# Storing two of three row tiles of an encoder step through 32x32 squares turned on VectorE, in 128-byte runs, instead of through TensorE transposes

## The chip, the core and the metric

The kernel runs on one core of one Trainium2 chip. A core has five engines with queues of their own: TensorE (PE, matrix products, with weight loads listed as PEld), VectorE (DVE), ScalarE (ACT), GpSimd (POOL) and SyncE (SP, which here only issues DMAs). Each engine works its queue in order; semaphores order the engines among each other. DMAs are issued from SP's, ACT's or POOL's queue and run on 16 DMA engines that all queues share. The metric is the device time of one execution, in microseconds (us); lower is better.

## The reference

Two groups of rows go through the same two layers with the same weights: a prompt of 1024 rows and a sample of 32 rows, each row 1024 wide, all in float32.

```python
def trunk(x, c, pool_cache, ...):
    for i in range(DEPTH):                         # DEPTH = 2
        mod = jax.nn.silu(c) @ w_ada[i] + b_ada[i]
        sh1, sc1, gt1, sh2, sc2, gt2 = jnp.split(mod[:, None, :], N_MOD, axis=-1)
        h = rmsnorm(x, g_norm[i, 0]) * (1 + sc1) + sh1
        ...                                        # layer 0: gated MLP over chunks, layer 1: pooling
        x = x + gt1 * rmsnorm(mix, g_norm[i, 1])
        h = rmsnorm(x, g_norm[i, 2]) * (1 + sc2) + sh2
        f = jnp.square(jax.nn.relu(h @ ffn_w_up[i])) @ ffn_w_down[i]
        x = x + gt2 * rmsnorm(f, g_norm[i, 3])
    return x, sgu_states, pool_states
```

What matters here is the very end: the last line of layer 1 for the prompt's first 768 rows, and how these rows get from the core's memory to `y_prompt` (1, 1024, 1024).

## The kernel before, in words

**Layout.** The 1056 rows are cut into three tiles (`TILES`): tile 0 and tile 1 with 384 prompt rows each, tile 2 with 256 prompt rows and the 32 sample rows (288 columns). On the core everything is held transposed: `acc[t]` is 128 partitions x 8 blocks x rows, so that column `r` of block `k` holds channels `128k` to `128k + 127` of row `r`. `A(t, k)` is block `k` of it.

**The FFN.** The hidden width 4096 is cut into eight chunks of 512 (`c` from 0 to 7). `ffn_item` does one chunk for one tile: four up blocks (`pf`, 24 matmuls each) whose results go through ACT (relu L1368, square L1370, a rounded copy `fh` L1192) and DVE (the rest `fl`), and then eight down blocks (`pg`, 12 matmuls each, three for each of four hidden blocks), each of which DVE adds to `acc`. Every product takes three matmuls (L932 to L934): high part by high part, by low part, and low by high. The down half of an item is held back and put behind the first up block of the next item (`pending`, `flush`), so that ACT and DVE have time for `fh` and `fl`. A weight comes in by an SP DMA into one of three `raw` buffers, ACT makes the high part `wh`, DVE the low part `wl`.

**The last passes.** In layer 1 chunks 6 and 7 are done for tiles 0 and 1 first and for tile 2 alone afterwards. So the results of tiles 0 and 1 can be stored while tile 2's last two chunks run, and only tile 2's own end stands at the end of the kernel.

**Fillers.** Work that is not on the main path is written as generators. `to_out` adds one per tile (`out_0`, `out_1`, `out_2`) as soon as that tile's last chunk is done. `weave` takes steps from the fillers whenever a running estimate of DVE's time is behind one of PE's (`time`, `tick`, `on_dve`); `yield 0.5` closes a filler for that long by the same estimate, `yield True` asks for the next step at once. The order within each engine's queue is then set by the framework from this program order and its own estimates.

**The end of tiles 0 and 1.** `residual` (L821) scales and adds: it reads the old `x` back from memory (`xd`, L828) and leaves the final result in `acc[t]`, still transposed. Then, for each of three blocks of 128 rows, eight 128x128 matmuls against the identity turn it on PE (L1700, into PSUM tiles `yT`), ACT copies the halves into a `raw` buffer `yo` (L1701), and SP stores 128 rows of 4 KB (L1702).

**The end of tile 2** has a path of its own (`last`). Its `acc` is turned on PE as it becomes ready (`turn_last`, L1449). The old `x` comes back in row order: `mix_to_ffn` had written it to `xtd`, `load_last` (L1423) reads it in runs of 128 bytes, and `turn_x` turns it in 32x32 squares on DVE. Four additions on DVE and four stores on SP finish the prompt rows (L1677, L1678). For the 32 sample rows ACT scales (L1682, `zlast`), POOL adds (L1683, `xlast`) and ACT's queue stores (L1684).

**Rooms.** `room("h", t)` and `room("l", t)` are the two large buffers of a tile; each new tile of that name waits until the one before it is no longer used. `hh` and `hl`, the FFN's inputs, live there.

**Other users of the queues touched.** Before this point POOL has done little: four DMAs at the start (`load_vectors`, L192) and eight memsets in layer 0. SP carries the weight loads (L436), the residual's reads (L828) and `load_last`.

Of the kernel before, what the change touches and what calls it, by code (L numbers as in the profile page):

```python
# [11 lines left out]
AF = mybir.ActivationFunctionType  # L12
# [3 lines left out]
P = 128  # L16
D = 1024
KB = D // P
# [5 lines left out]
HALO = 16  # L24
NV = 2

TILES = [(0, 384, 0), (384, 384, 0), (768, 256, DEC)]
# [7 lines left out]
def tile_stream_encoder_step(  # L35
# [25 lines left out]
    nc = tc.nc  # L61
    act = nc.scalar.activation
# [6 lines left out]
    def tick(us):  # L69
        time["pe"] += us  # L70
        time["dve"] = max(time["dve"], time["pe"] - 4.0)

    def on_dve(op, fixed, rate):
        def run(out, *args, **kw):
            n = 1
            for k in out.shape[1:]:
                n *= k
            time["dve"] += fixed + n / rate
            return op(out, *args, **kw)  # L79

        return run
# [4 lines left out]
    turn32 = on_dve(nc.vector.transpose, 0.1, 930.0)  # L86

    def pool(name, **kw):
# [14 lines left out]
    acc = [const.tile([P, KB, HALO + n], F32, name=f"acc{t}") for t, n in enumerate(ncol)]  # L103
# [7 lines left out]
    ident = const.tile([P, P], F32, name="ident")  # L111
# [6 lines left out]
        out=quad, in_=ident.rearrange("p (c m) -> p m c", m=32), op=ALU.add, axis=AX.X  # L118
# [9 lines left out]
    def A(t, kb, c0=0, w=None):  # L128
        w = ncol[t] - c0 if w is None else w
        return acc[t][:, kb, HALO + c0 : HALO + c0 + w]  # L130


    def room(part, t, name, dtype=F32):
        return work.tile([P, KB, ncol[t]], dtype, tag=f"h{part}{t}", bufs=1, name=name)
# [4 lines left out]
    def ps_dn(name):  # L139
        return psum.tile([P, 512], F32, tag="pd", bufs=3, name=name)  # L140

    def ps_ms(name):
        return psum.tile([P, 512], F32, tag="pm", bufs=3, name=name)
# [10 lines left out]
    def t_st(name):  # L154
        return work.tile([P, 4], F32, tag="st", bufs=6, name=name)
# [6 lines left out]
    def t_x(name, shape):  # L162
        return work.tile(shape, F32, tag="x3", bufs=3, name=name)

    def t_raw(name):
        return work.tile([P, 1024], F32, tag="raw", bufs=RAW_SLOTS, name=name)
# [501 lines left out]
    def need_ada(l, which):  # L668
        k = max(ada_last[(l, which * 4 + i)] for i in range(4))
        while state["next"] <= k:  # L670
            assert stream_ready()
            stream_step()
        run_deferred(True)
# [147 lines left out]
    def residual(st, l, cf, tag, out, store=True, stat=True):  # L821
        t = st.t
        n = ncol[t]
        xos = {}

        def load(k2):
            xos[k2] = t_x(f"xo_{tag}_{k2}", [P, 2, n])
            nc.sync.dma_start(xos[k2], xd[t][:, 2 * k2 : 2 * k2 + 2, :])  # L828

        got = []  # L830
        yield from st.finish(got)
        r = got[0]
        st2 = Stat(t, tag + "x")
        for half in range(2):
            for k2 in (2 * half, 2 * half + 1):
                load(k2)
            for k2 in (2 * half, 2 * half + 1):
                for k in (2 * k2, 2 * k2 + 1):
                    for c0, w, v in segs[t]:
                        a = A(t, k, c0, w)  # L840
                        stt(
                            out=a,
                            in0=a,
                            scalar=coef[:, l, cf, v, k : k + 1],
                            in1=r[:, c0 : c0 + w],
                            op0=ALU.mult,
                            op1=ALU.mult,
                        )
                    yield True
                a = acc[t][:, 2 * k2 : 2 * k2 + 2, HALO:]  # L850
                tt(out=a, in0=a, in1=xos[k2], op=ALU.add)
                if stat:
                    st2.square(2 * k2, a)
                yield k2 % 2 == 0
        if store:
            nc.sync.dma_start(xd[t], acc[t][:, :, HALO:])
        out.append(st2)
# [585 lines left out]
    def turn_last(d):  # L1443
        half = d // 4
        for i, (c0, _, _) in enumerate(LAST):
            if d % 4 == 0:
                take = ps_up if half == 0 and i < 2 else (ps_ms if half == 0 or i < 2 else ps_dn)
                last_ps[(i, half)] = take(f"yT{i}_{half}")
            nc.tensor.transpose(  # L1449
                last_ps[(i, half)][:, (d % 4) * P : (d % 4 + 1) * P], A(NT - 1, d, c0, P), ident  # L1450
            )
# [182 lines left out]
    run_ffn(0, to_pool)  # L1634


    def to_out(st):
        t = st.t
        col0, npr, nsm = TILES[t]
        blocks = [  # L1640
            (c * P, P, y_prompt[0, col0 + c * P : col0 + (c + 1) * P, :]) for c in range(npr // P)
        ]
        if nsm:
            blocks.append((npr, nsm, y_sample[0]))

        def last():

            turn_last(KB - 2)
            pn = ps_dn("pn_last")
            nb = len(LAST)  # L1650
            for k in (0, KB - 1):
                if k > 0:
                    turn_last(KB - 1)
                for i, (c0, _, _) in enumerate(LAST):
                    mm(
                        pn[:, 2 * i : 2 * i + 2],
                        st.sq[:, k, c0 : c0 + P],
                        ones[:, 0:2],
                        start=k == 0 and i == 0,
                        stop=k > 0 and i == nb - 1,  # L1660
                        skip_group_check=True,
                    )
            sums = pn[:, : 2 * nb].rearrange("p (b c) -> p b c", c=2)[:, :, 0]
            r, q = (t_st(f"{x}_last")[:, :nb] for x in ("r", "q"))
            act(out=r, in_=sums, func=AF.Abs_reciprocal_sqrt, scale=1.0 / D)
            tt(out=q, in0=r, in1=r, op=ALU.mult)
            stt(out=q, in0=sums, scalar=-0.5 / D, in1=q, op0=ALU.mult, op1=ALU.mult)
            stt(out=r, in0=q, scalar=1.5, in1=r, op0=ALU.add, op1=ALU.mult)
            xt = last_ps["x"]
            dsts = [dst for _, _, dst in blocks]  # L1670
            for i, (_, r0, nr) in enumerate(LAST):
                rows = slice(r0, r0 + nr)
                for half in range(2):
                    d = slice(half * 512, half * 512 + 512)
                    y, x = last_ps[(i, half)][rows, :], xt[rows, i, d]
                    if nr == P:
                        stt(out=x, in0=y, scalar=r[rows, i : i + 1], in1=x, op0=ALU.mult, op1=ALU.add)  # L1677
                        nc.sync.dma_start(dsts[i][:, d], x)  # L1678
                        continue

                    z = t_x(f"zlast{half}", [P, 512])[rows, :]
                    act(out=z, in_=y, func=AF.Copy, scale=r[rows, i : i + 1])  # L1682
                    nc.gpsimd.tensor_tensor(out=x, in0=z, in1=x, op=ALU.add)  # L1683
                    nc.scalar.dma_start(dsts[i][:, d], x)  # L1684
            yield False

        def run():
            need_ada(1, 5)
            if t == NT - 1:
                yield from last()  # L1690
                return
            yield from residual(st, 1, 3, f"r2_1_{t}", [], store=False, stat=False)
            yield 0.5
            for c0, w, dst in blocks:
                tick(1.0)
                yo = t_raw(f"yo{t}_{c0}")
                for half in range(2):
                    pt = ps_ms(f"yT{t}_{c0}_{half}")
                    for i in range(4):
                        nc.tensor.transpose(pt[:w, i * P : (i + 1) * P], A(t, half * 4 + i, c0, w), ident)  # L1700
                    act(out=yo[:w, half * 512 : (half + 1) * 512], in_=pt[:w, :], func=AF.Copy)  # L1701
                nc.sync.dma_start(dst, yo[:w, :])  # L1702
                yield False

        fillers.append((f"out_{t}", run()))

    run_ffn(1, to_out)
    flush()
    for t in range(NT):
# [44 lines left out]
```

## Time and profile before

| | us |
|---|---|
| median of three runs | 2160.07 (2159.87 to 2161.8) |
| the profiled execution | 2160.34 |
| its span, first to last instruction | 2158.5 |
| ACT busy with L1701, tiles 0 and 1 | 6.35 |
| a PE transpose of L1700, mean length of the 48 | 0.276 |

The granted TensorE clock was 0.998 in this execution. A profile row gives an engine, a line, an operation and its operands as out<-in; times in a timeline are microseconds from the start of the span, first the start and then the length. On PE successive instructions overlap, so that the lengths add up to more than the time that passes; the distance between two starts is what an instruction takes from the queue. DVE's elementwise work goes through one helper and shows as L79.

### The profile page before, as it was taken

To read this page: it belongs to the slowest core of one execution; us is meant where nothing else is said; L and a number is where in the kernel's file an instruction comes from. 1 tells how busy PE (TensorE), PEld (TensorE's weight loads), DVE (VectorE), ACT (ScalarE), POOL (GpSimd) and SP (SyncE) were. 2 spreads that over 40 slices of the span, in tenths; PEclk is the share of its full clock that TensorE was granted. 3 is DMA by queue.
4 is the path that set the end of the run, shared out by engine and by line. 5 is a ranking of instruction groups with operands and counts; after the bars stand their busy time and mean duration, and the time that the engine had idled before them with its cause. 6 is when DMAs were issued, how large, how long until landed. Compare 5 with 4: busy or idle time off the path is not lost.

```text
span 2158.5 us, 33202 instructions
## 1 busy us (share of the span) xinstructions
PE 2140.5 (99%) x13186; PEld 2077.4 (96%) x13186; DVE 1428.4 (66%) x2531; ACT 982.7 (46%) x1667; POOL 7.9 (0%) x20
## 2 busy tenths in 40 slices
PE   8999999999999999999999999999999999999998
PEld 5878999999999999999999999999999999999998
DVE  6778838567778549576757779869684553523375
ACT  5634431233456652324345566656464542322454
POOL 0000000000000000000000000000000000000000
PEclk9999999999999999999999999999999999999999
DMA  8586524353446444334545466465454541302243
GB/s 289 163 259 208 181 82 136 97 163 109 121 134 213 128 146 147 101 114 141 178 125 162 147 194 198 145 193 164 141 164 131 165 149 57 108 20 69 79 137 120
DMA packets 372495, 311.78 MB, mean 144 GB/s; under 512 B 29842, under 2 KB 335290, under 8 KB 372340
## 3 DMA queue, kind: packets, MB, share of 16 engines
q1 hardware_dynamic: 372084, 309.43, 46.6%
q8 instruction: 103, 1.69, 0.3%
q14 instruction: 52, 0.43, 0.1%
q10 hardware_dynamic: 128, 0.14, 0.0%
q0 software_dynamic: 128, 0.09, 0.0%
HBM read 278.95 MB, written 30.66 MB: 143 GB/s over the span
## 4 chain that ended last, share of the span: by engine, by line
PE 97%; DVE 1%; DMA 1%; ACT 1%; issue 0%; POOL 0%; POOLq 0%; SPq 0%; ACTq 0%; DVEq 0%
PE pf L932 11%; PE pf L934 11%; PE pf L933 11%; PE pg L932 11%; PE pg L934 11%; PE pg L933 11%; PE pu L932 3%; PE pu L934 3%; PE pu L933 3%; PE po L932 3%; PE po L933 3%; PE po L934 3%; PE pv L958 2%; PE pv L960 2%; PE pv L959 2%; PE psp L1286 1%
## 5 line engine op out<-in xcount | busy, mean ns | idle before, releaser
L932 PE MATMUL pg<-fh,wh_dn 128*128 128x384 f32 (+1 forms) x1536 | 496.0, 323 | 0.0
L932 PE MATMUL pf<-hh,wh_up 128*128 128x384 f32 (+1 forms) x1536 | 494.4, 322 | 0.0
L934 PE MATMUL pf<-hh,wl_up 128*128 128x384 f32 (+1 forms) x1536 | 493.0, 321 | 1.2 <-DVE wl_up L79 1.2
L933 PE MATMUL pf<-hl,wh_up 128*128 128x384 f32 (+1 forms) x1536 | 493.1, 321 | 0.0
L933 PE MATMUL pg<-fl,wh_dn 128*128 128x384 f32 (+1 forms) x1536 | 492.5, 321 | 0.0
L934 PE MATMUL pg<-fh,wl_dn 128*128 128x384 f32 (+1 forms) x1536 | 492.5, 321 | 0.0
L79 DVE TENSOR_TENSOR wl_up<-raw,wh_up 128x1024 fp32r<-128x1024 f32 x152 | 186.0, 1224 | 169.9 <-ACT wh_up L449 167.5
L449 ACT ACTIVATE wh_up<-raw 128x1024 fp32r<-128x1024 f32 x152 | 161.1, 1060 | 283.9 <-PE pf L933 218.1
L934 PEld LDWEIGHTS pf<-hh,wl_up 128*128 128x128 f32 x1536 | 288.6, 188 | 1.9 <-DVE wl_up L79 1.9
L932 PEld LDWEIGHTS pg<-fh,wh_dn 128*128 128x128 f32 x1536 | 288.3, 188 | 1.3 <-ACT fh L1192 0.4
L933 PEld LDWEIGHTS pg<-fl,wh_dn 128*128 128x128 f32 x1536 | 288.3, 188 | 0.9 <-DVE fl L79 0.2
L933 PEld LDWEIGHTS pf<-hl,wh_up 128*128 128x128 f32 x1536 | 288.3, 188 | 0.4
L932 PEld LDWEIGHTS pf<-hh,wh_up 128*128 128x128 f32 x1536 | 288.2, 188 | 0.4
L934 PEld LDWEIGHTS pg<-fh,wl_dn 128*128 128x128 f32 x1536 | 288.3, 188 | 0.0
L79 DVE TENSOR_TENSOR acc<-acc,pg 128x384 f32<-128x384 f32 (+1 forms) x336 | 174.2, 519 | 150.5 <-PE pg L934 149.8
L449 ACT ACTIVATE wh_dn<-raw 128x1024 fp32r<-128x1024 f32 x152 | 160.9, 1060 | 207.9 <-PE pg L933 170.6
L79 DVE TENSOR_TENSOR wl_dn<-raw,wh_dn 128x1024 fp32r<-128x1024 f32 x152 | 186.0, 1224 | 82.0 <-ACT wh_dn L449 81.6
L79 DVE SCALAR_TENSOR_TENSOR aa<-raw,csil,aa 128x512 f32<-128x512 f32 (+1 forms) x364 | 204.1, 623 | 5.3 <-DMA raw<-in_w_ada_dram 5.0
L1368 ACT ACTIVATE r<-pf 128x384 f32<-128x384 f32 (+1 forms) x192 | 86.6, 451 | 197.9 <-PE pf L934 178.7
L79 DVE TENSOR_TENSOR fl<-r,fh 128x384 fp32r<-128x384 f32 (+1 forms) x192 | 100.4, 523 | 85.8 <-ACT fh L1192 84.3
L932 PE MATMUL pu<-hh,wh_u 128*128 128x384 f32 (+1 forms) x384 | 126.0, 328 | 0.0
L932 PE MATMUL po<-ush,wh_o 128*128 128x384 f32 (+1 forms) x384 | 123.5, 322 | 0.0
(276 smaller groups left out, 2925.0 us busy)
## 6 DMA issues: line engine op xcount, KB each, us to landing
raw<-in_ffn_w_up_dram SPq DMA_DIRECT2D x152, 512.0 KB, 3.8
raw<-in_ffn_w_down_dram SPq DMA_DIRECT2D x152, 512.0 KB, 3.5
raw<-in_w_ada_dram SPq DMA_DIRECT2D x96, 512.0 KB, 4.2
raw<-in_sgu_w_in_dram SPq DMA_DIRECT2D x40, 512.0 KB, 4.0
xd<-acc SPq DMA_DIRECT2D x8, 1536.0 KB, 8.0
raw<-in_sgu_w_out_dram SPq DMA_DIRECT2D x24, 512.0 KB, 3.6
xo_r<-xd SPq DMA_DIRECT2D x32, 384.0 KB, 3.3
vd<-vt SPq DMA_DIRECT2D x32, 256.0 KB, 4.2
```

Source lines behind the costliest of these rows:

```text
L79: return op(out, *args, **kw)
L449: act(out=wh, in_=r, func=AF.Copy)
L932: mm(ps[:, :n], wh, rh, start=i == 0, stop=False)
L933: mm(ps[:, :n], wh, rl, start=False, stop=False)
L934: mm(ps[:, :n], wl, rh, start=False, stop=i == last)
L958: mm(ps[:m, :], a_h, wh[:, o : o + 512], start=k == 0, stop=False)
L959: mm(ps[:m, :], a_h, wl[:, o : o + 512], start=False, stop=False)
L960: mm(ps[:m, :], a_l, wh[:, o : o + 512], start=False, stop=k == KB - 1)
L1286: mm(sp[:, c * P : (c + 1) * P], vl[:, c, k * P : (k + 1) * P], wr[:, c * P : (c + 1) * P], start=True, stop=True,)
L1368: act(out=r[:, :n], in_=ps[:, :n], func=AF.Relu)
```

## The change

Tiles 0 and 1 are no longer turned on PE. After `residual`, the new generator `turned` takes a buffer (`room("h", 1)` for tile 0, `room("l", 1)` for tile 1) and has DVE turn `acc[t]` in 32x32 squares, 32 rows at a time: twelve instructions of 128 partitions x 8 blocks x 32 for a tile. A square swaps 32 channels with 32 rows, so the buffer then has, on partition `32a + m`, for rows `32i + m` of the tile, the channels `128k + 32a` to `128k + 32a + 31`: 32 channels side by side, which is a run of 128 bytes. The rows are stored straight from there: for each block `k` and each group of partitions `a` one DMA of 32 x 12 runs, 32 DMAs a tile. All go by POOL's queue, except twelve of tile 1 (`a` even, `k` below 6), which go by SP's. The PSUM tiles `yT`, ACT's copies, the `raw` buffers `yo` and the six large stores go away, and with them the `yield 0.5` ahead of them and a microsecond of estimated PE time for each block. Tile 2's path is unchanged.

```diff
+    def turned(t, room_of):
+
+        col0, npr, _ = TILES[t]
+        sq = room(*room_of, f"y_sq{t}").rearrange("p k n -> p (k n)")
+        for i in range(npr // 32):
+            turn32(
+                sq[:, 256 * i : 256 * i + 256].rearrange("p (k s) -> p k s", k=KB),
+                acc[t][:, :, HALO + 32 * i : HALO + 32 * i + 32],
+            )
+            yield i % 2 == 0
+
+        y = y_prompt[0, col0 : col0 + npr, :].rearrange("(i m) c -> m i c", m=32)
+        for k in range(KB):
+            for a in range(4):
+                x = sq[32 * a : 32 * a + 32].rearrange("p (i k s) -> p i k s", k=KB, s=32)
+                c = k * P + 32 * a
+                queue = nc.sync if t == 1 and a % 2 == 0 and k < 6 else nc.gpsimd
+                queue.dma_start(y[:, :, c : c + 32], x[:, :, k])
+
     def to_out(st):
...
             yield from residual(st, 1, 3, f"r2_1_{t}", [], store=False, stat=False)
-            yield 0.5
-            for c0, w, dst in blocks:
-                tick(1.0)
-                yo = t_raw(f"yo{t}_{c0}")
-                for half in range(2):
-                    pt = ps_ms(f"yT{t}_{c0}_{half}")
-                    for i in range(4):
-                        nc.tensor.transpose(pt[:w, i * P : (i + 1) * P], A(t, half * 4 + i, c0, w), ident)
-                    act(out=yo[:w, half * 512 : (half + 1) * 512], in_=pt[:w, :], func=AF.Copy)
-                nc.sync.dma_start(dst, yo[:w, :])
-                yield False
+            yield from turned(t, ("h", 1) if t == 0 else ("l", 1))
```

## The prediction

> **What bounds the kernel now.** I read first the page's head, then the end of the chain of waits, then TensorE's (PE's) timeline around the lines that go.
>
> ```profile
> span 2158.5 us, 33202 instructions
> PE 2140.5 (99%) x13186; PEld 2077.4 (96%) x13186; DVE 1428.4 (66%) x2531; ACT 982.7 (46%) x1667; POOL 7.9 (0%) x20
> ```
>
> PE is busy all the way, so an instruction taken from PE's queue shortens the run by its slot, as long as PE finds nothing late behind it. The end of the chain of waits (start, us, what) shows what follows PE's last work:
>
> ```profile
> 2151.78 0.69 ACT zlast L1682
> 2152.60 1.27 POOL xlast L1683
> 2153.86 1.23 POOLq L1750
> ```
>
> The last step is on GpSimd (POOL): two additions for the 32 sample rows, and then their stores. From 2152.60, where POOL begins, to the end of the span are 5.9 us. So two things have to be there for the end: PE's results, and a POOL that is free to take them.
>
> The profiled execution took 2160.34 us, 1.84 over its span; the median of the runs is 2160.07, 0.27 less. I make the sum on the span and give times against the median, that is span plus 1.57.
>
> **What goes from PE.** PE's timeline (start, length, engine, line, operation) at the 24 transposes of tile 0 and the 24 of tile 1:
>
> ```profile
> 2105.48 1.47 PE L1700 MATMUL yT<-ident,acc 128*128 128x128 f32 x12
> ...
> 2106.92 0.30 PE L933 MATMUL pg<-fl,wh_dn 128*128 128x288 f32 x1
> ...
> 2108.11 0.30 PE L933 MATMUL pg<-fl,wh_dn 128*128 128x288 f32 x1
> 2108.61 1.14 PE L1700 MATMUL yT<-ident,acc 128*128 128x128 f32 x8 [0.20 <-ACT yo L1701]
> ...
> 2109.72 0.29 PE L932 MATMUL pg<-fh,wh_dn 128*128 128x288 f32 x1
> ...
> 2113.80 0.60 PE L1700 MATMUL yT<-ident,acc 128*128 128x128 f32 x4
> 2114.16 0.42 PE L808 MATMUL pn_rf<-sc_rf,ones 128*128 128x384 f32 x1
> ...
> 2131.16 1.47 PE L1700 MATMUL yT<-ident,acc 128*128 128x128 f32 x12
> 2132.79 0.66 PE L1700 MATMUL yT<-ident,acc 128*128 128x128 f32 x4 [0.15 <-ACT yo L1701]
> ...
> 2133.68 1.07 PE L1700 MATMUL yT<-ident,acc 128*128 128x128 f32 x8
> ...
> 2134.72 0.30 PE L933 MATMUL pg<-fl,wh_dn 128*128 128x288 f32 x1
> ```
>
> Starts count, since lengths overlap. Nine pg matmuls from 2106.92 to 2108.11 make 0.13 each. Tile 0: 2105.48 to 2106.92 holds twelve transposes and one pg, 1.44 - 0.13 = 1.31; 2108.11 to 2109.72 holds eight, two pg and a wait for ACT, 1.61 - 0.26 = 1.35; the last four take 0.36. Sum 3.0. Tile 1: 2131.16 to 2134.72 holds all 24 with their waits and four pg: 3.56 - 0.52 = 3.0. Together **6.1 us** leave PE. The twelve ACT copies (L1701) and six stores (L1702) go too; ACT and SP have idle time there, so I count nothing for them except that ACT reaches the next item sooner.
>
> **What takes the transposes' place on PE.** At 2131.16 they stood between tile 2's last up block (pf of chunk 7) and its down blocks, which need that block's fh (ACT: relu, square, copy) and fl (DVE). They covered that wait. PE's first matmul after the block before it, and ACT's three steps for that block:
>
> ```profile
> 2127.97 0.30 PE L932 MATMUL pf<-hh,wh_up 128*128 128x288 f32 x1
> ```
>
> ```profile
> 2128.16 0.41 ACT L1368 ACTIVATE r<-pf 128x288 f32<-128x288 f32 x1 [1.84 <-PE pf L934]
> 2128.61 0.44 ACT L1370 ACTIVATE r<-r 128x288 f32<-128x288 f32 x1
> 2129.08 0.45 ACT L1192 ACTIVATE fh<-r 128x288 fp32r<-128x288 f32 x1
> ```
>
> From 2128.16 to 2129.53 are 1.37 us, and relu starts 0.2 after PE has gone on: fh comes 1.57 after that. In the changed order PE has eleven other matmuls first (nine of output block 0, two of block 1), 1.44 us, so it waits 0.1 to 0.2. The first matmul with fl comes five later, at about 2.3 us; fl stands on DVE behind seven of the new squares. By the estimate of the next part these start at 2127.9 and take 2.5, and fl itself about 0.45, as ACT's copy: 2130.9, which is 2.8 after PE's slot at 2131.16 - 3.0 = 2128.1. That is 0.5 to 0.6 more. In all I give back **0.8**: at least 0 (DVE a little earlier than I think), at most 3.0, when the whole cover of tile 1 is lost. I take a value near the low end, because eleven matmuls already stand in the gap. Tile 0's 24 covered nothing: behind them come pg blocks with inputs done earlier.
>
> **DVE: 24 squares of 128x256 added.** The nearest row is a group of the same shape in the other direction:
>
> ```profile
> L79 DVE STREAM_TRANSPOSE acc<-x_rows 128x256 f32<-128x256 f32 x9 | 3.7, 433 | 0.0
> ```
>
> The stretches in which they fall (length; busy time of PE, weight loads, DVE, ACT, POOL), and the end of tile 1's residual on DVE's timeline:
>
> ```profile
> 2093.50:2103.00 9.50, 9.50 (x74) 9.50 (x73) 6.75 (x9) 6.47 (x12) 0.00 (x0) 1.00 0.68 190
> ...
> 2117.00:2131.00 14.00, 14.00 (x107) 14.00 (x107) 13.51 (x23) 3.74 (x8) 0.00 (x0) 1.00 0.36 108
> ```
>
> ```profile
> 2130.09 0.95 DVE L79 TENSOR_TENSOR acc<-acc,xo_r 128x768 f32<-128x768 f32 x1
> ```
>
> One takes 0.43, back to back less, about 0.35: 4.2 to 5.2 us a tile. Tile 0's fall into 2093.5 to 2103, where DVE has 2.75 idle and where what is queued behind them are weight halves used a pass later and fl blocks used from 2105 on; they end near **2103**. Tile 1's follow its residual, which in the changed order starts some 3 us earlier (no transposes of tile 0 ahead of it) and ends near 2127.5 instead of 2131; with one fl ahead of them and an fl and accumulations between them they end near **2133.5**. DVE is full from 2117 to 2131, so this is where a late fl comes from; it is in the 0.8. Both times are estimates from the order of DVE's queue and these durations, good to a microsecond.
>
> **The stores: 64 DMAs of 384 runs of 128 bytes.** 32 of tile 0 and 20 of tile 1 go by POOL's queue, 12 of tile 1 by SP's. On POOL, the two final additions stand behind all 52. What a POOL DMA costs its engine, the trace shows only at the start, for 96, 8 and 16 runs:
>
> ```profile
> 2.34 0.54 POOL L192 DMA_DIRECT2D row<-in_b_ada_dram  x1
> 2.87 0.52 POOL L192 DMA_DIRECT2D row<-in_pool_scale_dram  x1
> 3.38 0.51 POOL L192 DMA_DIRECT2D row<-in_sgu_g_v_dram  x1
> ```
>
> From issue to landing the first of these took (last number, us):
>
> ```profile
> row<-in_b_ada_dram POOLq DMA_DIRECT2D x1, 48.0 KB, 5.3
> ```
>
> SP's price for 256 runs of 128 bytes in three dimensions (ns, least, median, most):
>
> ```profile
> L431 SPq DMA_DIRECT2D x_rows<-in_x_prompt_dram x32: 565/607/1701, 35.9 to 57.8; - x32
> ```
>
> - SP: 12 x 0.61 = 7.3 us from 2133.5, done by 2141. SP's next work are the final stores at about 2147, and nothing is queued in between: hidden, up to 1.1 each.
> - POOL: call its price per DMA x. Lower end 0.51. From 16 to 96 runs it rises by 0.026; carried on to 384 this gives 0.63. If instead all of the 0.54 for 96 runs is per run, 384 take 2.15: the upper end. A DMA also waits for the landing of the eighth before it, which at 5.3 us would make 0.66. I take **0.63**, since an eighth of the runs costs nearly the same.
> - POOL is asked for its additions at 2152.60 - 5.3 = 2147.3. Tile 0's 32 take 20 us from 2103, so POOL is free again at 2123. Tile 1's 20 take 12.6 from 2133.5, to 2146.1: just in time. So POOL costs nothing at x up to 0.69, then 2 us per 0.1; above 0.95 tile 0's are still running at 2133.5, and it is 5.2 us per 0.1.
>
> The Trainium skill, "DMA: Bandwidth & Descriptors", section Anatomy of one DMA, says that many descriptors can be emitted before their generation shows; the three rows agree, up to 96 runs, and no row of this case goes further.
>
> **The sum.** -6.1 (PE) + 0.8 (late fh and fl) + 0 (POOL, SP, DMA) = **-5.3 us**: 2154.8, or -0.25%.
>
> **Rivals.**
> 1. *POOL becomes the bound* (slower). Its place: the additions behind 52 DMAs. They start at 2103 + 52x, and the time is that plus 5.9 plus 1.57. At x = 0.954 it equals the time before; at 1.04 it is 0.2% slower; at 1.25 it is 2175.5; at 2.15 it is 2222. Between 0.75 (2156.0) and 1.03 it eats the gain without a measurable loss. For it: 384 runs are four times the largest DMA that POOL has in this trace, and in three dimensions. Against it: the nearly flat rows above.
> 2. *The DMA engines drain short stores slowly* (slower). The trace has short reads only (xraw, 128-byte runs, in 2063.0 to 2066.5), and the page's mean for all packets of SP's queue:
>
> ```profile
> DMA packets 1927, 0.24 MB, mean 70 GB/s; under 512 B 1927, under 2 KB 1927, under 8 KB 1927
> q1 hardware_dynamic: 1927, 0.24, 44.2%
> ```
>
> ```profile
> q1 hardware_dynamic: 372084, 309.43, 46.6%
> ```
>
> That is 0.442 x 3.5 us x 16 / 1927 = 12.8 ns of an engine per short read, and 43 ns for a mean packet (832 bytes). Tile 1's 32 DMAs put 768 packets on each of 16 engines: 9.8 us at 12.8 ns, done by 2143.5, and 33 us at 43 ns, which holds the final stores back to 2166.5 and gives 2166.5 + 6 + 1.57 = 2174. It decides from 25 ns on. I take a value near 13, as the size is the same. The Trainium skill, the same page, section Specifications, says that below 512 bytes the engine reads, modifies and writes, which would make a short store dearer than a short read; no row here shows a short store.
> 3. *PE only changes what it waits for.* If fl comes as late as the 24 transposes of tile 1 took, only tile 0's 3 us stay: 2157.0, no measurable change. For it: DVE is full from 2117 to 2131. Against it: the eleven matmuls in the gap.
>
> **How the numbers follow.** What a measurement can tell from no change is about 0.2%, 4.3 us. Forecast 0.42, its own range 2153.6 to 2156. Rival 1 with x above 1.04: 0.26; with x from 0.75 to 1.03: 0.16 (same). Rival 2: 0.10 (slower). Rival 3: 0.06 (same). So faster 0.42, same 0.22, slower 0.36. The range runs from the best forecast, 2153.6, where nothing is given back on PE, to 2175, where rival 1 stands at x = 1.25; 0.05 lies below, 0.15 above.
>
> **What would show it.** Right: no yT of L1700, zlast near 2151.78 - 5.3 = 2146.5; the 24 squares at 0.43 or less; POOL's DMAs at 0.6 to 0.7 each; the additions waiting for zlast, as before, near 2147.3. Wrong: additions that start right behind POOL's last DMA, late (rival 1); POOL in time, but stores landing long after their issue and a DMA share near 1 after 2133 (rival 2); a gap on PE before the first pg of chunk 7 (rival 3). The weakest step is x, taken from DMAs a quarter as large at most.

## The result, and the profile after

| | before | after |
|---|---|---|
| median of five runs | 2159.87 us (2158.64 to 2161.8) | 2178.18 us (2176.93 to 2180.9) |
| the profiled span | 2158.5 | 2176.4 |

The ratio is 1.0088, 95% interval 1.0077 to 1.0099: the changed kernel is slower by 18.3 us, where 5.3 less was forecast, and it lies above the range. The head of the page of the changed kernel:

```profile
span 2176.4 us, 33168 instructions
PE 2135.2 (98%) x13138; PEld 2072.3 (95%) x13138; DVE 1435.4 (66%) x2555; ACT 975.8 (45%) x1655; POOL 40.0 (2%) x72
```

PE has 48 instructions less and 5.3 us less of busy time, as meant. The end of the chain of waits (start, us, what) is no longer ACT's `zlast` but POOL's own stores:

```profile
2168.73 0.97 issue
2169.71 0.62 POOL out_dram L1654
...
2171.02 1.32 POOLq L1759
2172.34 1.23 POOL xlast L1702
```

The timeline around PE's end shows that everything else was ready far earlier (the first row of each engine's last work: the row norms, the scaled sample rows, SP's final stores):

```profile
2144.28 0.17 ACT L1684 ACTIVATE r_last<-pn_last 128x3 f32<-128x3 f32 x1 [0.17 <-PE pn_last L1674]
...
2145.21 1.25 ACT L1701 ACTIVATE zlast<-yT,r_last 32x512 f32<-32x512 f32 x2 [0.76 <-DVE r_last L79]
...
2145.93 2.31 SPq L1697 DMA_DIRECT2D out_dram<-xlast  x4
```

In the kernel before, `r_last` was at 2150.86 and the additions at 2152.60. Now `r_last` comes 6.6 us sooner and the additions 18.5 us later, at 2171.08. So 25 us of waiting for POOL stand between them. POOL's timeline (start, length, engine, line, operation, count, and in brackets the idle time before it):

```profile
2102.36 1.27 POOL L1654 DMA_DIRECT2D out_dram<-y_sq  x2 [1529.34 <-DVE y_sq L79]
2105.32 1.22 POOL L1654 DMA_DIRECT2D out_dram<-y_sq  x2 [1.68 <-issue]
2110.11 1.23 POOL L1654 DMA_DIRECT2D out_dram<-y_sq  x2 [3.57 <-issue]
...
2127.18 1.23 POOL L1654 DMA_DIRECT2D out_dram<-y_sq  x2 [1.07 <-issue]
2129.48 1.23 POOL L1654 DMA_DIRECT2D out_dram<-y_sq  x2 [1.06 <-issue]
...
2169.71 1.31 POOL L1654 DMA_DIRECT2D out_dram<-y_sq  x2 [0.97 <-issue]
2171.08 2.48 POOL L1702 TENSOR_TENSOR xlast<-zlast,xlast 32x512 f32<-32x512 f32 x2
```

The rhythm is two stores, a pause, two stores, a pause. A pair comes every 2.30 us (2127.18 to 2129.48), though its two instructions take 1.23. The pause is put down to "issue", which means that the profile shows nothing that POOL waits for. The rows of the buffers `y_sq` (least, median, most in ns; first and last start), and the time from a store's issue to its landing:

```profile
L1654 POOL DMA_DIRECT2D out_dram<-y_sq x52: 615/616/643, 2102.4 to 2170.4; - x52
L79 DVE STREAM_TRANSPOSE y_sq<-acc x24: 400/403/439, 2092.7 to 2131.7; 128x256 f32<-128x256 f32 x24
L1654 SPq DMA_DIRECT2D out_dram<-y_sq x12: 337/477/498, 2132.1 to 2137.7; - x12
...
DMA to landing us min/median/max: 1.8/2.0/4.5
```

The 52 stores take 0.616 us each, 32.0 in all; the stretch from 2102.36 to 2171.08 is 68.7. More than half of it, some 36 us, is pauses. A store lands (the trace records its completion) 2.0 us after its issue in the median: the store at 2127.18 lands at 2129.17, and the next but one begins at 2129.48, 0.31 us later. By the trace's starts and landings this holds throughout: from the third store on, none begins sooner than 0.30 us after the landing of the second before it, and 44 of these 50 begin 0.31 to 0.36 us after it. So each POOL store waits until the second one before it has landed; no more than two are in flight, that is issued and not yet landed.

### The profile page after: what moved, and what is told of

The parts are those of the page before. It is cut to its first block, busy times and chain, and to the rows that moved or that the text cites. A ratio compares the mean times of both kernels' runs of the same rounds, so it can differ in the third digit from the quotient of the medians.

```text
span 2176.4 us, 33168 instructions
## 1 busy us (share of the span) xinstructions
PE 2135.2 (98%) x13138; PEld 2072.3 (95%) x13138; DVE 1435.4 (66%) x2555; ACT 975.8 (45%) x1655; POOL 40.0 (2%) x72
## 4 chain that ended last, share of the span: by engine, by line
PE 96%; DVE 1%; issue 1%; DMA 1%; POOL 1%; ACT 0%; POOLq 0%; SPq 0%; DVEq 0%; ACTq 0%
PE pf L932 11%; PE pg L932 11%; PE pf L934 11%; PE pf L933 11%; PE pg L934 11%; PE pg L933 11%; PE pu L932 3%; PE pu L934 3%; PE pu L933 3%; PE po L932 3%; PE po L934 3%; PE po L933 3%; PE pv L958 2%; PE pv L960 2%; PE pv L959 2%; PE psp L1286 1%
```

## The experiments

What had to be told apart: is the loss POOL's queue (rival 1) or slow DMA engines (rival 2)? And if it is the queue, what makes the pauses: the memory that the kernel sets aside for the descriptors of POOL's DMAs (`dynamic_dma_scratch_size=1024`, near the kernel's end), the number of DMAs in flight, or something else that stops POOL? The kernel before was timed again beside each group of experiments, with medians of 2158.67, 2158.80 and 2159.12 us; the ratios below are to these.

**Tile 1 by SP alone**

```diff
-                queue = nc.sync if t == 1 and a % 2 == 0 and k < 6 else nc.gpsimd
+                queue = nc.sync if t == 1 else nc.gpsimd
```

> All 32 stores of tile 1 go by SP, tile 0's 32 stay on POOL. Theory A (POOL's queue holds two of these DMAs, so a pair goes every 2.3 us, and the additions stand behind them): POOL's 32 are done when the 32nd of the changed kernel was, at about 2146.3, the additions start there, and the time is 2146.3 + 5.9 + 1.57 = 2154, about 24 below the changed kernel and 6 below the kernel before. SP's 32 take 0.5 each, 2132 to 2148, and its four final stores come some 2 us later than in the changed kernel, which is hidden if they land by 2152. Theory B (short stores hold up the DMA engines, whichever queue they come from): SP's stores or the final stores land late, and the time stays near 2170 or above.

Measured: 2164.35 us, ratio to the kernel before 1.0025 (1.0016 to 1.0035). POOL did what theory A says, and its additions came at once behind its last store. But SP's 32 stores took 25 us instead of 16. Rows of the timeline, for POOL, ACT's queue and SP's queue:

```profile
2146.99 2.49 POOL L1702 TENSOR_TENSOR xlast<-zlast,xlast 32x512 f32<-32x512 f32 x2
2148.28 1.56 ACTq L1703 DMA_DIRECT2D out_dram<-xlast  x2
...
2132.08 25.06 SPq L1654 DMA_DIRECT2D out_dram<-y_sq  x32
2157.24 1.89 SPq L1697 DMA_DIRECT2D out_dram<-xlast  x4
```

The waits of SP's queue from 2130 on (total, times, longest) name the reason:

```profile
SPq L1654 <- DMA out_dram<-xlast: 8.2, 2, 7.9
```

SP stood 7.9 us in front of its 19th store until a store of ACT's queue, issued behind POOL's addition, had landed. In the trace the DMAs of SP and ACT signal the same eight semaphores in turn, and a DMA waits until the one that used its semaphore before it has landed: the 19th store has the semaphore of ACT's store of 2148.28, which lands at 2149.91, and begins at 2149.93. So this is not theory B. The DMA view of 2148 to 2154, when SP's short stores ran beside little else, prices them:

```profile
q1 hardware_dynamic: 2400, 0.30, 30.2%
```

That is 0.302 x 6 us x 16 / 2400 = 12.1 ns of an engine for a run of 128 bytes.

**The same stores in halves**

```diff
-                queue.dma_start(y[:, :, c : c + 32], x[:, :, k])
+                cuts = [(0, 12)] if queue is nc.sync else [(0, 6), (6, 12)]
+                for i0, i1 in cuts:
+                    queue.dma_start(y[:, i0:i1, c : c + 32], x[:, i0:i1, k])
```

> Each POOL DMA is cut in two of 192 runs: 104 DMAs instead of 52, the same bytes and runs; SP's stay whole. Theory A1 (what is limited is the memory for descriptors, room for some 800 runs): four are in flight, they come in groups of four or evenly, and the 104 take 60 to 70 us, done by 2163 to 2173: a time near that of the changed kernel, 2165 to 2180. Theory A2 (what is limited is the number of DMAs, two in flight): they come in pairs as before, 104 x 1.0 to 1.15 = 104 to 120 us, done at 2206 to 2222: a time of 2213 to 2230. If the price of an issue by itself were the limit (0.62 for 384 runs, little less for 192): 104 x 0.5 to 0.6 without pauses, done at 2154 to 2165.

Measured: 2176.13 us. POOL's timeline now begins in fours, and the rows of `y_sq` give the price of one:

```profile
2098.05 2.28 POOL L1656 DMA_DIRECT2D out_dram<-y_sq  x4 [1526.65 <-DVE y_sq L79]
2100.98 2.35 POOL L1656 DMA_DIRECT2D out_dram<-y_sq  x4 [0.66 <-issue]
2105.09 2.28 POOL L1656 DMA_DIRECT2D out_dram<-y_sq  x4 [1.77 <-issue]
```

```profile
L1656 POOL DMA_DIRECT2D out_dram<-y_sq x104: 565/565/588, 2098.0 to 2168.0; - x104
```

Four are in flight instead of two: from the fifth store on, none begins sooner than 0.30 us after the landing of the fourth before it, and most begin before the third has landed. So it is not a count of DMAs that is limited (A2 falls) but what they carry: four times 192 runs fit, a fifth does not. The time hardly changes, because half a store costs nearly as much of POOL as a whole one (0.565 against 0.616): the issues take 104 x 0.565 = 58.8 us instead of 32.0, while the pauses fall from 34.8 to 10.6.

**The memory for descriptors, as it is and doubled**

Both kernels free room in the same way; the second has one more line changed.

```diff
-        bb = sgu.tile([P, P], F32, tag="bs", bufs=2, name=f"bs{g}")
-        with tc.issue_after(loads[("v", 2, 3)]):
-            nc.sync.dma_start(bb, sgu_b_s[0, g].partition_broadcast(P))
+        bb = wt
...
-                if g % 2 == 0:
-                    wg = t_x(f"wg{t}_{g}", [P, 2, 256])
-                else:
-                    wg = late.tile([P, 2, 256], F32, tag="wg", bufs=1, name=f"wg{t}_{g}")
+                wg = t_x(f"wg{t}_{g}", [P, 2, 256])
...
-        "TRN2", target_bir_lowering=False, num_devices=1, dynamic_dma_scratch_size=1024
+        "TRN2", target_bir_lowering=False, num_devices=1, dynamic_dma_scratch_size=2048
```

> Control for e3_ring128. To free room in SBUF it leaves out the load of the gate's bias b_s (another loaded tile stands in its place, so the output isn't the reference's), and takes the last wg buffers from another pool. The memory for POOL's descriptors stays at 1024. Every theory: pairs every 2.3 us as in the changed kernel, POOL's last store at about 2170, time within 3 us of 2178.

> As e3_ring64 (b_s left out), with the memory for POOL's descriptors doubled, 1024 to 2048. Theory A1 (the memory holds two of these DMAs; doubled, it holds four or five, and a DMA takes 2.3 us from start to landing against 0.62 for its issue): no pauses, tile 0's 32 done at about 2122.5, tile 1's 20 from 2132 to 2144.5, the additions wait for zlast as in the kernel before, near 2146.1: time 2153.5, 24 below the control. Theory A2 (two DMAs in flight, whatever the memory) and theory C (the pause is POOL held up by another engine or by the DMA engines): pairs every 2.3 us as in the control, time within 3 us of it.

Measured: 2177.68 us for the control and 2153.19 with the memory doubled, ratio to the kernel before 0.9974 (0.9963 to 0.9986). POOL's timeline of the control, and below it of the doubled one:

```profile
2126.84 1.24 POOL L1648 DMA_DIRECT2D out_dram<-y_sq  x2 [1.07 <-issue]
2129.15 1.23 POOL L1648 DMA_DIRECT2D out_dram<-y_sq  x2 [1.07 <-issue]
```

```profile
2101.45 4.91 POOL L1648 DMA_DIRECT2D out_dram<-y_sq  x8 [1530.03 <-DVE y_sq L79]
...
2113.53 7.35 POOL L1648 DMA_DIRECT2D out_dram<-y_sq  x12 [1.43 <-issue]
...
2131.54 5.49 POOL L1648 DMA_DIRECT2D out_dram<-y_sq  x9 [5.58 <-DVE y_sq L79]
...
2145.05 2.50 POOL L1696 TENSOR_TENSOR xlast<-zlast,xlast 32x512 f32<-32x512 f32 x2 [0.29 <-ACT zlast L1695]
```

Stores of 0.615 stand in rows of five to twelve, tile 0's are done before tile 1's are there (at 2126.0 instead of the 2122.5 expected, since a few pauses stay), and the additions wait for ACT again, as in the kernel before. The sum of POOL's pauses (total, times, longest), the control first:

```profile
POOL out_dram L1648 <- issue: 34.8, 32, 3.6
```

```profile
POOL out_dram L1648 <- issue: 5.9, 5, 2.7
```

One line differs between the two, and the pairs that A2 and C expected are gone: A1 holds. Where a store of the second kernel still pauses for "issue", it begins 0.31 us after the landing of the fifth before it, so five are in flight. It also bears out the rest of the forecast: without the long pauses the time is 5.5 us below the kernel before (2158.67 beside it), where 5.3 was forecast. (What both kernels leave out is worth 0.5 us by the control, 2177.68 against 2178.18, which is within the spread of the runs.)

**The final additions on DVE**

```diff
-                    nc.gpsimd.tensor_tensor(out=x, in0=z, in1=x, op=ALU.add)
+                    nc.vector.tensor_tensor(out=x, in0=z, in1=x, op=ALU.add)
```

> The two final additions are done by DVE instead of POOL, so nothing stands behind POOL's stores but the end of the program; all 64 stores stay as in the changed kernel. The queue's rate (a pair every 2.3 us) is untouched, so POOL's last store still starts near 2170.4 and lands some 2.3 us after its start. Expected by the theory that the rate of POOL's queue sets the end: a span of 2173 to 2174 and a time of 2174.5 to 2176, only 2 to 4 below the changed kernel. If the place of the additions behind the stores were the whole loss: about 2154 to 2160.

Measured: 2175.18 us. DVE adds as soon as it can, and POOL goes on storing (rows of both timelines):

```profile
2147.58 1.29 DVE L1702 TENSOR_TENSOR xlast<-zlast,xlast 32x512 f32<-32x512 f32 x2
```

```profile
2170.18 0.61 POOL L1654 DMA_DIRECT2D out_dram<-y_sq  x1 [0.32 <-issue]
```

What stands behind the stores on POOL is worth 3 us. The rest is the stores themselves.

**One tile alone**

In each, the other tile keeps its transposes, copies and three stores of the kernel before.

```diff
-            yield from turned(t, ("h", 1) if t == 0 else ("l", 1))
+            if t == 0:                             # the second kernel: t == 1
+                yield from turned(t, ("h", 1) if t == 0 else ("l", 1))
+                return
+            yield 0.5
+            for c0, w, dst in blocks:
...
```

> Only tile 0 is turned by DVE and stored by POOL (32 DMAs); tile 1 keeps its 24 transposes on PE and its six... three stores of whole rows by SP. POOL's 32 are done near 2146.9, and PE, with only tile 0's 3.0 us gone, asks for the additions at 2152.6 - 3.0 = 2149.6: POOL is in time. Expected: 2160.0 - 3.0 = 2157, and no wait for fh or fl at the last down block, since tile 1's transposes cover it again. If 32 stores on POOL were already too many: additions right behind POOL's last store, and a time above 2157.

> Only tile 1 is turned; tile 0 keeps its transposes. POOL has 20 DMAs, the first near 2134.5, as tile 1's squares end, SP 12. At a pair every 2.3 us, with one longer pause near 2141 and one near 2149, POOL is done at 2134.5 + 20 x 1.15 + 2 = 2159 to 2160, 10 us after zlast (2149.5). Expected: 2160 + 5.3 + 1.6 = 2166 to 2167. At the predicted 0.63 a DMA without pauses POOL would be done at 2147.1, in time, and the kernel would take 2157.

Measured: 2156.48 us with tile 0 alone (ratio 0.9991, 0.9982 to 1.0), 2169.38 with tile 1 alone. The 32 stores of tile 0 are done 1.6 us before POOL is asked for the additions:

```profile
2146.05 1.24 POOL L1654 DMA_DIRECT2D out_dram<-y_sq  x2 [1.06 <-issue]
2148.85 2.49 POOL L1702 TENSOR_TENSOR xlast<-zlast,xlast 32x512 f32<-32x512 f32 x2 [1.56 <-issue]
```

The 20 of tile 1 are not, though they are fewer, because they start late:

```profile
2136.04 1.27 POOL L1654 DMA_DIRECT2D out_dram<-y_sq  x2 [1563.93 <-DVE y_sq L79]
...
2162.00 2.49 POOL L1702 TENSOR_TENSOR xlast<-zlast,xlast 32x512 f32<-32x512 f32 x2
```

26 us for 20 stores, 1.30 each. The expectation was 2.4 us short, of which 1.5 is the start (2136.0 instead of 2134.5, since tile 0's transposes are still ahead on PE).

**Two versions that move the stores**

First, tile 1 on SP as above, and the stores of the sample rows taken off ACT's queue:

```diff
-                    nc.scalar.dma_start(dsts[i][:, d], x)
+                    nc.gpsimd.dma_start(dsts[i][:, d], x)
```

> As e1_sp32 (tile 1's 32 stores on SP), and the two stores of the 32 sample rows go by POOL's queue behind its additions instead of ACT's. In e1_sp32 SP stood for 7.9 us in front of its 19th store until a store of ACT's queue had landed; with ACT's stores gone from that rotation this wait should go. Expected: SP's 32 from 2132 without a long gap, 0.51 each, done at 2148.5; its four final stores to 2151, landed at 2153; POOL's additions at 2147 as in e1_sp32, its two last stores issued by 2151 and landed by 2153. Time 2154 to 2156, below the kernel before. If SP's stores are slow in themselves (short stores, no wait for another queue): SP done near 2157 as before, time near 2164.

Measured: 2157.20 us, ratio 0.9990 (0.9981 to 0.9998). SP's long wait is gone, 32 stores in 17.52 us:

```profile
2132.47 17.52 SPq L1654 DMA_DIRECT2D out_dram<-y_sq  x32
2150.09 1.93 SPq L1697 DMA_DIRECT2D out_dram<-xlast  x4
```

The time was 1 to 3 us above what was expected. SP's stores took 0.55 us each instead of 0.51, so that its four final stores began only at 2150.09, behind them, and the last landed at 2154.4; POOL's additions began at 2147.48, each is followed by a store that POOL issues itself, and the last of these landed at 2153.8. Both were expected by 2153. Second, tile 0's last twelve stores on SP ahead of tile 1's squares, 24 of tile 1's on SP, and the sample rows' stores on POOL's queue as in the first:

```diff
+    rest_of_0 = []
...
+        while t == 1 and rest_of_0:
+            nc.sync.dma_start(*rest_of_0.pop(0))
...
+                if t == 0 and k >= 5:
+                    rest_of_0.append((y[:, :, c : c + 32], x[:, :, k]))
+                    continue
-                queue = nc.sync if t == 1 and a % 2 == 0 and k < 6 else nc.gpsimd
+                queue = nc.sync if t == 1 and k < 6 else nc.gpsimd
```

> Built from what the runs showed. Tile 0: 20 stores on POOL at once, the other 12 on SP, issued just before tile 1's squares, where SP's queue has little to do. Tile 1: 24 on SP, 8 on POOL. The two stores of the 32 sample rows go by POOL's queue, as in e8_sp32_pool. At a pair every 2.3 us and the longer pauses seen, POOL is done with tile 0 near 2131 and with tile 1 near 2144; SP is done with tile 1 at 2132.2 + 24 x 0.53 = 2145. Then zlast (near 2146) is what the additions wait for, and the four final stores start as their rows are ready. Expected: a span near 2152.5 and a time of 2153.5 to 2154.5, 2.5 to 3.5 below e8_sp32_pool. If POOL's own two last stores still cost what they did there (additions at 2146, 3.6 us for both with their issues, 2.3 to land): 2153.5 all the same, since they start 1.5 us earlier; if the time stays at 2157, something other than POOL's and SP's queues sets it.

> The same kernel a second time, one look: the same time within 2 us.

Measured: 2154.20 us, ratio to the kernel before 0.9976 (0.9966 to 0.9987), and 2154.70 in the one further run. The ends of POOL's and SP's timelines:

```profile
2143.76 0.63 POOL L1661 DMA_DIRECT2D out_dram<-y_sq  x1 [2.10 <-PE pg L934]
2146.73 1.27 POOL L1709 TENSOR_TENSOR xlast<-zlast,xlast 32x512 f32<-32x512 f32 x1 [2.35 <-issue]
```

```profile
2132.79 12.95 SPq L1661 DMA_DIRECT2D out_dram<-y_sq  x24
2146.63 2.31 SPq L1704 DMA_DIRECT2D out_dram<-xlast  x4
```

Both queues are empty before the final rows are ready, and the gain on PE becomes time: 0.24% less than the kernel before.

## Why the prediction was wrong, point by point

- **PE: -6.1 right, the give-back of 0.8 half as large.** DVE's last addition for tile 0 (before the first square) and `r_last` mark out PE's tail. In the kernel before (timelines of DVE and ACT; the row of `r_last` after stands above):

```profile
2093.08 0.55 DVE L79 TENSOR_TENSOR acc<-acc,pg 128x384 f32<-128x384 f32 x1
...
2150.86 0.17 ACT L1665 ACTIVATE r_last<-pn_last 128x3 f32<-128x3 f32 x1 [0.17 <-PE pn_last L1655]
```

```profile
2092.19 0.55 DVE L79 TENSOR_TENSOR acc<-acc,pg 128x384 f32<-128x384 f32 x1
```

  The second fence is the kernel after. The tail was 57.8 us and is 52.1: 5.7 less, where 5.3 was forecast. (The other 0.9 of `r_last`'s 6.6 is there before the first square.) With tile 0 alone the tail is 2.9 shorter, with tile 1 alone 2.7. The late `fh` and `fl` cost 0.4 instead of 0.8: `fl` is ready 2.3 us after PE's slot for the down blocks (2129.51 after 2127.17), where 2.8 was forecast. PE's timeline after, where a step is otherwise 0.13:

```profile
2128.49 0.29 PE L933 MATMUL pg<-fl,wh_dn 128*128 128x288 f32 x1
2128.79 0.40 PE L932 MATMUL pg<-fh,wh_dn 128*128 128x288 f32 x1
2129.03 0.30 PE L934 MATMUL pg<-fh,wl_dn 128*128 128x288 f32 x1
...
2129.56 0.40 PE L933 MATMUL pg<-fl,wh_dn 128*128 128x288 f32 x1
2129.80 0.30 PE L934 MATMUL pg<-fh,wl_dn 128*128 128x288 f32 x1
```

  The starts step by 0.30, 0.24 and 0.24, which is 0.39 more than three steps of 0.13. Rival 3 is excluded. (The range's lower end, 2153.6, does not come out of the sum: with nothing given back it is 2160.07 - 6.1 = 2154.0. Nothing else hangs on it.)
- **DVE: right, to 1.4 us.** A square takes 0.40 (0.35 to 0.43 forecast). Tile 0's end near 2102.1 (2103), tile 1's near 2132.1 (2133.5).
- **SP: right.** Twelve stores in 6.1 us (7.3), hidden.
- **POOL's price x: here it failed.** The step was "I take 0.63, since an eighth of the runs costs nearly the same". As the length of the instruction this was right: 0.616. As the time that a store holds the queue it was half of the truth: 68.7 us for 52, 1.32 each. So the sum's term of 0 for POOL was wrong; between the control and the doubled memory it is 24.5 us. The sentence ahead of it, "a DMA also waits for the landing of the eighth before it", had the right kind of limit with the wrong number. With the kernel's memory for descriptors it is the second before it, and 2.3 us (2.0 to landing and 0.31 after it) by two is 1.15. The rest of the 1.32 is late landings: up to 4.5 us where weight loads run, with a pause of 3.6; 3.4 and 2.6 for the stores issued at 2139.07 and 2140.02, with a pause of 2.1; and 3.7 beside SP's final stores, with one of 2.4.
- **Rival 1: right in place and formula, with x = 1.32.** It was given 0.26 for x above 1.04. The formula puts the additions at 2103 + 52 x 1.32 = 2171.6 (2171.08 measured) and the time at 2179.1 (2178.18). The range stopped at x = 1.25, so it missed the time by 3. The argument against the rival, three nearly flat rows, told nothing of a full queue: POOL has four small DMAs in that trace (the three, and one of 0.69 us ahead of them), which never fill it.
- **Rival 2: excluded.** 12.1 ns for a short store in the first experiment, next to the 12.8 that was taken from short reads, and far below the 25 from which it decides. A short store was no dearer than a short read.

What makes the pauses is shown from two sides: halves go in fours, and twice the memory takes the sum of the pauses from 34.8 to 5.9 us. The Trainium skill, "DMA: Bandwidth & Descriptors", section SWDGE vs HWDGE vs iDMA, says that GpSimd writes descriptors into rings in the core's own memory, from which the DMA engines drain them; the runs agree, and it does not say how many DMAs a ring holds. The same page, section Anatomy of one DMA, gives about 2.0 us plus the bytes by 436 GB/s for one such DMA, by which these 48 KB would take an estimated 2.1; the trace has 2.0. With that page and the kernel's line on the scratch size the question could have been put before the run; the trace of before alone could not answer it.

Left open: how the memory is counted (not by runs alone: 1024 bytes do not hold 5 x 192 = 960 runs, and 2048 hold 5 x 384 = 1920, exactly twice as many), and why the two stores near 2140 landed late, when no weight loads run. A larger memory in the changed kernel with nothing else altered was not run.

## What to carry to other kernels

The price of a DMA in a long row on GpSimd's queue was here the larger of two numbers: the length of its instruction, and the time to landing and 0.31 us more, divided by how many fit in flight. With whole stores that is 1.15 against 0.616, with halves, which land after 1.8, it is 2.1 / 4 = 0.53 against 0.565, and the halves mostly go without a pause. So for such a row look up the memory for descriptors as well as the instruction. Idle time before a DMA that is put down to "issue", in a steady rhythm, was such a full queue here. Before work is moved to an idle engine, see what stands behind it there: two additions of 1.25 us waited 25 us behind a POOL that was busy with its stores for less than half of the time (32.0 of 68.7 us).

## What the runs showed that was not expected

- With 1024 bytes set aside, POOL's queue holds two DMAs of 384 runs or four of 192, but not five; with 2048 it holds five of 384, and the pauses nearly vanish.
- An issue on POOL costs little more for more runs: 0.616 us for 384 runs, 0.565 for 192, 0.54 for 96.
- Stores on SP and on ACT's queue wait for each other through the semaphores that they share in turn: one store of ACT's, late, held SP for 7.9 us.
